# A decoder block on one core, its instruction order written out as a table

## The chip, the core and the metric

The kernel runs on one core of one Trainium2 chip. The metric is device time in microseconds from the start to the end of one execution. The core has a matrix engine (TensorE, shown as PE, with its weight loads as PEld), a vector engine (VectorE, DVE), a scalar and lookup engine (ScalarE, ACT), GpSimd (POOL), and SyncE (SP), which here only issues DMA transfers. Each engine works through its own list of instructions in order and waits at semaphores for the others. Transfers are issued by SP, ACT and POOL; a transfer that has to wait for its operand or its buffer holds up everything behind it on the engine that issues it. Matmul results go to PSUM, of which the kernel uses eight banks under the names ps_A, ps_B, ps_C and ps_D.

## What is computed

One decoder layer for 512 tokens of width 1024 in float32:

```python
h = h + 0.5 * swiglu(rmsnorm(h), ffn1_w1, ffn1_w3, ffn1_w2)   # hidden width 2816
z = rmsnorm(h) @ w_in             # 8 queries, 3 x (2 keys, 2 values), gates, S5 input u
o_nsa = nsa_attention(q, ...)     # 8 heads x 64: compressed, selected and window branch
o_s5  = s5_mixer(u, ...)          # 32 groups x 16 channels, 64 complex states, scan over 512
h = h + concat(o_nsa, o_s5) @ w_out
h = h + 0.5 * swiglu(rmsnorm(h), ffn2_w1, ffn2_w3, ffn2_w2)
h = h + sigmoid(rmsnorm(h) @ w_gate) * (p @ w_ple)            # p has width 256
out = rmsnorm(h)
```

With eight selected blocks out of eight the selected branch sees all earlier keys, so it is a causal attention like the window branch; the compressed branch attends to 31 pooled blocks. S5 is a linear recurrence, followed by gelu and a gated projection (GLU, `glu`).

## The kernel before

Activations stand transposed, channels on partitions and tokens in columns: `h` is eight tiles of 128x512. A product in float32 precision is made of three matmuls in the faster fp32r type: every operand is split into a rounded part and a rest (`hi` and `lo` for weights, `xh` and `xl` or `sh` and `sl` for activations, `hq` for hidden tiles), and hi*hi, hi*lo and lo*hi are added in PSUM. For each unit of 128x1024 weights this means a load (`raw<-in_wpack`, line 111), a cast on ACT (`hi<-raw`, line 152) and a subtraction on DVE (`lo<-raw,hi`, line 154). All matmuls go through one helper, line 131.

**Feed-forward.** 22 hidden tiles are made and consumed in four chunks (`CHUNKS`, `FFN_ORDER`): `up` makes a hidden tile, `down` adds a chunk's product to `h` (line 488). After the first seven tiles of the first feed-forward, and the first two of the second, the tiles are "fast" (`up_fast`): they use seven half products instead of eight, from sums and differences of weight halves. These sums are made by two accumulating transfers, which POOL issues (lines 362 and 368), and two DVE additions (lines 364 and 365); ACT's `ah` (line 370) and DVE's `al` (line 371) split the last. Partial products are copied between banks by ACT (lines 383 and 399), combined by DVE into `t3` (lines 422, 426 and 432, shown as `t` by the profile), and split into `hq` (lines 352 and 353).

**Mixer.** Queries, keys and values are projected and rotated; the rotated queries go to DRAM (`qd<-r`) and come back in another layout (`qf<-qd`, lines 1147 and 1148); keys and values for the compressed branch go the same way (`kcd`, `vcd`, then `cst`, lines 1044 and 1045). ACT copies the returned queries into `QA` and `QB` (lines 1149 and 1150). `scores` finds the row maxima of the scores; `values` then walks over 48 blocks of keys: score matmuls into ps_B or ps_C, one exponential into `e`, a second rounded one into `eh` (every third a DVE copy instead), a DVE subtraction `el` (line 1264), and two matmuls into ps_D. S5 runs beside it, with its state passed through DRAM by POOL (`si`, `so`). After the gelu of S5 (`yt`, line 871), `glu` multiplies by gate weights and `out_half(4-8)` projects S5's half of the output; `out_half(0-4)` projects attention's half when its last piece (`oh`, `ol`, lines 1275 and 1276) is ready.

**What sets the order.** The program is written with generators that are woven in fixed proportions (`weave`), with a few instructions pinned in place (`tc.keep_in_program_order`, `tc.issue_after`); from that, the framework's planner (`schedule_with_timeline_sim=True`) decides the order on each engine. Weight units are loaded by SP in the feed-forwards and by ACT in the mixer; the choice is this line:

```python
load_unit(i, q or (nc.sync if more else nc.scalar))
```

Raw units come from a ring of four buffers (a larger ring where `more` is set), so a load waits until the unit that had the buffer before has been split.

Of the kernel before, what the change touches and what calls it, by code (L numbers as in the profile page):

```python
# [76 lines left out]
def block_kernel(ctx: ExitStack, tc: tile.TileContext, a: dict, out: bass.AP):  # L77
# [22 lines left out]
    raws, loads = {}, {}  # L100
# [3 lines left out]
    def load_unit(i, q):  # L104
        w = UNIT_W[i]
        if more and i % (4 + more[1]) >= 4:
            raw = more[0].tile([128, UNIT], F32, tag="raw", name="raw", bufs=more[1])
        else:
            raw = ring.tile([128, UNIT], F32, tag="raw", name="raw", bufs=4)
        src = a["wpack"][128 * UNIT_OFF[i]:128 * UNIT_OFF[i + 1]].rearrange("(p c) -> p c", c=w)  # L110
        loads[i] = q.dma_start(raw[:, :w], src)
        raws[i] = raw
# [15 lines left out]
    pinned = tc.keep_in_program_order  # L128
# [7 lines left out]
    def unit(raw_only=False, keep=None, q=None, after=None):  # L136
        i = unit_i[0]
        unit_i[0] += 1
        w = UNIT_W[i]
        if i not in raws:  # L140
            load_unit(i, q or (nc.sync if more else nc.scalar))
        raw = raws.pop(i)
        if raw_only:
            return raw
        return split(raw, (slice(0, 512), slice(512, w)) if i == 0 else (slice(0, w),), keep, after)

    def split(raw, parts=(slice(0, UNIT),), keep=None, after=None):
# [3 lines left out]
        for c in parts:  # L151
            S.copy(hi[:, c], raw[:, c])  # L152
            with tc.issue_after(after.ins) if after else nullcontext():
                V.tensor_tensor(lo[:, c], raw[:, c], hi[:, c].bitcast(F32), OP.subtract)  # L154
# [11 lines left out]
    class Norm:  # L166
# [25 lines left out]
        def finish(self, pin=False):  # L192
            self.ri, pb = rsqrt_rows([self.acc], 4, pin)
            self.rb = npool.tile([128, SEQ], F32, tag="rb", name="rb", bufs=1)
            V.tensor_copy(self.rb, pb)
# [57 lines left out]
    class Scaled(Norm):  # L253
# [13 lines left out]
        def spread(self, tmp, xpool, pool, pb):  # L267
# [8 lines left out]
            def scale(k):  # L276
                pinned(V.scalar_tensor_tensor(row(k), h[:, k, :], gains[:, self.gi, k:k + 1], pb, OP.mult, OP.mult))
                S.copy(self.xh[:, k], row(k))

            for k in range(KT + 1):  # L280
                if k < KT:
                    scale(k)
                if k:
                    self.last = pinned(V.tensor_tensor(self.xl[:, k - 1], row(k - 1),
                                                       self.xh[:, k - 1].bitcast(F32), OP.subtract))
# [4 lines left out]
            def combine(n, a, b, op):  # L290
                t = tmp().rearrange("p a (b c) -> p (a b) c", c=256)
                with tc.issue_after(self.last.ins):
                    for i in range(2):
                        V.tensor_tensor(t[:, 2 * i:2 * i + 2], a(i), b(i), op)
# [12 lines left out]
    def rsqrt_rows(parts, nb, pin=False):  # L307

        steps = rsqrt_steps(parts, nb, pin)
# [3 lines left out]
    def rsqrt_steps(parts, nb, pin=False, pin_last=False):  # L313
        st = bank("D", (128, 4))[:, :nb]
        for b in range(nb):
            for i, t in enumerate(parts):
                p = mm(st[:, b:b + 1], t[:, b * 128:(b + 1) * 128], ones[:, 0:1], i == 0, i == len(parts) - 1)
                if pin and b + i == 0:
                    pinned(p)
# [11 lines left out]
        p = mm(pb, ones, dg.rearrange("p b t -> p (b t)"), True, True)  # L331
        if pin_last:
            pinned(p)
# [10 lines left out]
    def ffn(nrm, done, plain, xp, hp, fp, bg=None, first=None, restate=None):  # L344
        fast = not bg
        if True:
# [88 lines left out]
            def up(f):  # L435
                if f >= plain:
                    return up_fast(f, f + 1 < FT_N and f not in [c[0] for c in CHUNKS[1:]])
                after = nrm.last if fast and f == 0 else None
                wu = [first if f == 0 and first else unit(), unit(after=after)]
                z = [bank("C"), bank("C")] if f == 2 else [bank("A"), bank("B")]  # L440
                both = [(j, k) for j in range(2) for k in range(KT)]
                if after:
# [29 lines left out]
            def aside(n, mark=None):  # L472
                for _ in range(n if bg else 0):
                    with tc.issue_after(mark.ins) if mark else nullcontext():
                        next(bg, None)

            def down(fl, last):
                n = len(fl)
                cur = None
                for m in range(KT):  # L480
# [7 lines left out]
                    mark = V.scalar_tensor_tensor(h[:, m, :], o, 0.5, h[:, m, :], OP.mult, OP.add)  # L488
# [5 lines left out]
                    if not last:  # L494
                        aside((2 - m % 2) * (m > 4 or fl[0] > 0), mark)
# [18 lines left out]
    def s5_constants(sp):  # L514
        if True:
# [10 lines left out]
            late(bx, a["s5_b"])  # L526
            cx = sp.tile([128, 2, NG, 16], F32, name="cx")
            late(cx, a["s5_c"])
            dk = sp.tile([16, NG], F32, name="dk")
            late(dk, a["s5_dT"])  # L530
            sgn = sp.tile([128, 2], F32, name="sgn")
            late(sgn, a["sgn"])
# [275 lines left out]
    def mixer(ctx):  # L808
# [50 lines left out]
        table = []  # L859

        def act(*args, **kw):
            with tc.issue_after(table[0].ins):
                S.activation(*args, **kw)  # L863

        def gelu2(o, x, w, tag):

            t = tp.tile([128, SEQ], F32, tag=tag, name="gt")[:, :w]
            act(t, x, AF.Square)
            V.scalar_tensor_tensor(t, t, 1 / 0.044715, x, OP.add, OP.mult)
            act(t, t, AF.Tanh, scale=math.sqrt(2 / math.pi) * 0.044715)  # L870
# [146 lines left out]
        def v_gates():  # L1017
# [18 lines left out]
            act(gp1, gp1, AF.Exp)  # L1036
# [60 lines left out]
        def glu():  # L1097
# [4 lines left out]
            for m in range(4):  # L1102
# [8 lines left out]
                act(sg, o, AF.Tanh, scale=0.25, bias=bglu[:, m:m + 1])  # L1111
# [23 lines left out]
        def scores(qb, env, pool, tags="B", stage=("ra", "ra")):  # L1135
# [24 lines left out]
            for j, (h0, b0) in enumerate((h0, b0) for half in range(2) for b0 in range(0, 2, nb)  # L1160
# [9 lines left out]
                for i in range(n):  # L1170
                    for r in range(nb):
                        act(s_[:, i, r], s_[:, i, r], AF.Exp, bias=mc[:, i, r:r + 1], accum_out=dc[:, i, r:r + 1])
                yield

        def compressed(*qbs):

            for qb in qbs:
# [14 lines left out]
                act(ec, ec, AF.Exp)  # L1192
# [38 lines left out]
        def values(qb, env):  # L1231
# [3 lines left out]
            for g in range(2):  # L1235
# [5 lines left out]
                for i, (br, kb) in enumerate(blocks):  # L1241
# [16 lines left out]
                    act(e, st, AF.Exp)  # L1258
                    if i % 3 == 2:
                        V.tensor_copy(eh, e)  # L1260
                    else:
                        act(eh, st, AF.Exp)
# [41 lines left out]
        table.append(tc.keep_in_program_order(S.preload_act_table_set("exp_and_others")))  # L1304
# [80 lines left out]
    norm2 = rsqrt_steps([n2.acc], 4, True, True)  # L1385
    for m in range(KT):
# [23 lines left out]
    with tc.tile_pool(name="gate", bufs=2, reuse_waits="tile") as gp:  # L1410
# [12 lines left out]
        for hf in range(2):  # L1423
            cs = slice(hf * HS, hf * HS + HS)
            for i in range(KT):
# [8 lines left out]
                if i == 0 and hf == 0:  # L1434
                    ng.finish(True)
# [37 lines left out]


# [149 lines left out]
```

## Time and profile before

| | us |
|---|---|
| median of 3 runs | 1095.41 (1093.74 to 1097.05) |
| the profiled execution | 1096.0 |
| its span, first to last instruction | 1094.2 |
| TensorE busy in the span | 1042.1 |
| VectorE busy | 794.0 |
| ScalarE busy | 516.8 |
| GpSimd busy | 92.7 |
| mean granted TensorE clock | 0.985 of full |

The views used below are these. The page's first part gives each engine's busy time. A table by stretches gives, for each piece of the span, the busy time of every engine with its number of instructions, the granted clock, the busy share of the DMA engines and the rate. Waits are listed by engine, tile and source line, with the instruction that ended them: "PE ps_A L131 <- DVE yt L871: 5.8, 1, 5.8" means that matmuls into ps_A waited 5.8 us in all, once, at longest 5.8 us, for DVE's `yt` of line 871. The chain of waits goes back from the last instruction, each step to what released it. In timeline rows a bracket such as [5.87 <-ACT ps_B L863] gives the idle time before the instruction and what ended it. Matmuls are pipelined, so their shown length is longer than their spacing.

### The profile page before, as it was taken

Reading aid. Unit: us, or ns where it says so; the run is one execution under the profiler, and the core shown is the slowest. Engines: PE = TensorE matmul, PEld = TensorE weight load, DVE = VectorE, ACT = ScalarE, POOL = GpSimd, SP = SyncE. Lnnn points to the kernel's source line nnn. Section 1 sums busy time; section 2 is a strip of 40 time slices with the busy share of each in tenths; the row PEclk is TensorE's granted clock in tenths of the full one; section 3 lists DMA queues with packets and bytes.
Section 4 is the critical chain, followed back from the end, with each engine's and each line's share of the span. In section 5 each row is a group of like instructions: output and inputs, shape, how many; then the busy total and the mean of one; then the engine's idle time right before and its main releaser. Section 6 shows DMA issues by size and latency. Waiting matters only on the chain.

```text
span 1094.2 us, 16835 instructions
## 1 busy us (share of the span) xinstructions
PE 1042.1 (95%) x6446; PEld 897.5 (82%) x6446; DVE 794.0 (73%) x1339; ACT 516.8 (47%) x911; POOL 92.7 (8%) x118
## 2 busy tenths in 40 slices
PE   6999999998999999979799999999999999999996
PEld 4887999798889788767377668799899899898895
DVE  6999786786787766777468887976477557566766
ACT  5334255344435423346647875555255245255541
POOL 5000010000000200010000001011010101000000
PEclk9999999999999999989899999999999999999998
DMA  9334366786657737773621026256365635535302
GB/s 284 137 99 112 81 166 171 192 200 153 166 130 187 234 97 226 216 218 111 187 68 40 0 97 173 77 146 176 84 144 142 177 73 143 171 96 153 111 8 77
DMA packets 86625, 151.14 MB, mean 138 GB/s; under 512 B 27648, under 2 KB 47104, under 8 KB 86544
## 3 DMA queue, kind: packets, MB, share of 16 engines
q1 hardware_dynamic: 66352, 98.11, 29.5%
q0 software_dynamic: 13152, 29.66, 13.7%
q10 hardware_dynamic: 7040, 22.29, 6.5%
q8 instruction: 50, 0.82, 0.3%
q14 instruction: 31, 0.25, 0.1%
HBM read 123.27 MB, written 17.83 MB: 129 GB/s over the span
## 4 chain that ended last, share of the span: by engine, by line
PE 62%; ACT 4%; issue 3%; DVE 3%; DMA 3%; ACTq 0%; SPq 0%; POOLq 0%; POOL 0%; DVEq 0%
PE ps_A L131 18%; PE ps_C L131 18%; PE ps_B L131 17%; PE ps_D L131 10%; DMA qf<-qd 2%; ACT e L863 1%; ACT eh L863 1%; ACT ps_B L863 1%; DMA raw<-in_wpack 1%; DVE el L1264 0%; DVE lo L154 0%; ACT hi L152 0%; DMA qd<-r 0%; ACT QA L1149 0%; ACT pt L1270 0%
## 5 line engine op out<-in xcount | busy, mean ns | idle before, releaser
L152 ACT CAST hi<-raw 128x1024 fp32r<-128x1024 f32 (+2 forms) x201 | 206.0, 1041 | 245.8 <-PE ps_C L131 103.5
L154 DVE TENSOR_TENSOR lo<-raw,hi 128x1024 fp32r<-128x1024 f32 (+2 forms) x201 | 240.0, 1218 | 70.8 <-ACT hi L152 66.4
L131 PE MATMUL ps_C<-hq,hi 128*128 128x512 f32 x704 | 218.0, 392 | 3.9 <-ACT hq L352 2.3
L131 PEld LDWEIGHTS ps_C<-hq,hi 128*128 128x128 f32 x704 | 130.4, 188 | 32.9 <-ACT hq L352 3.2
L131 PE MATMUL ps_A<-xh,hi 128*128 128x256 f32 (+1 forms) x456 | 141.0, 311 | 7.4 <-ACT xh L175 6.3
L131 PE MATMUL ps_A<-xl,hi 128*128 128x256 f32 (+1 forms) x456 | 141.2, 312 | 3.1 <-DVE xl L176 2.1
L131 PE MATMUL ps_A<-xh,lo 128*128 128x256 f32 (+1 forms) x456 | 140.9, 310 | 1.7 <-DVE lo L154 1.7
L131 PE MATMUL ps_C<-hq,lo 128*128 128x512 f32 x352 | 136.2, 390 | 0.0
L131 PEld LDWEIGHTS ps_A<-xh,hi 128*128 128x128 f32 x456 | 86.4, 190 | 12.7 <-ACT xh L175 6.2
L131 PEld LDWEIGHTS ps_A<-xl,hi 128*128 128x128 f32 x456 | 86.2, 190 | 11.6 <-DVE xl L176 4.7
L131 PEld LDWEIGHTS ps_A<-xh,lo 128*128 128x128 f32 x456 | 86.4, 190 | 6.2 <-DVE lo L154 1.9
L131 PE MATMUL ps_B<-sh,hi 128*128 128x256 f32 x280 | 79.1, 283 | 2.7 <-ACT ps_B L399 2.7
L131 PE MATMUL ps_B<-sh,lo 128*128 128x256 f32 x280 | 78.8, 281 | 0.7 <-DVE lo L154 0.7
L131 PE MATMUL ps_B<-sl,hi 128*128 128x256 f32 x280 | 78.9, 282 | 0.0
L131 PEld LDWEIGHTS ps_C<-hq,lo 128*128 128x128 f32 x352 | 66.1, 188 | 13.6
L362 POOL DMA_DIRECT2D raw<-in_wpack x35 | 30.4, 869 | 483.7 <-DVE h L1127 168.3
L488 DVE SCALAR_TENSOR_TENSOR h<-ps_C,h 128x512 f32<-128x512 f32 x64 | 43.9, 689 | 36.8 <-PE ps_C L131 36.4
L131 PE MATMUL ps_D<-sh,hi 128*128 128x256 f32 x220 | 61.7, 283 | 0.4 <-ACT hi L152 0.4
L131 PE MATMUL ps_D<-sh,lo 128*128 128x256 f32 x220 | 61.7, 281 | 0.0
L131 PE MATMUL ps_D<-sl,hi 128*128 128x256 f32 x220 | 61.3, 281 | 0.0
L131 PE MATMUL ps_B<-xh,hi 128*128 128x512 f32 (+1 forms) x164 | 57.9, 353 | 0.9 <-ACT hi L152 0.9
L131 PE MATMUL ps_B<-xh,lo 128*128 128x512 f32 (+1 forms) x160 | 56.0, 350 | 0.8 <-DVE lo L154 0.8
(402 smaller groups left out, 2327.4 us busy)
## 6 DMA issues: line engine op xcount, KB each, us to landing
raw<-in_wpack SPq DMA_DIRECT2D x132, 512.0 KB, 4.3
raw<-in_wpack ACTq DMA_DIRECT2D x40, 512.0 KB, 4.2
raw<-in_wpack POOLq DMA_DIRECT2D x35, 256.0 KB, 4.2
raw<-raw POOLq DMA_DIRECT2D x35, 256.0 KB, 3.4
so<-s5o POOLq DMA_DIRECT2D x8, 768.0 KB, 5.9
si<-s5i POOLq DMA_DIRECT2D x8, 512.0 KB, 5.6
h<-in_xT SPq DMA_DIRECT2D x8, 256.0 KB, 5.5
s5i<-fs SPq DMA_DIRECT2D x4, 512.0 KB, 4.6
```

Source lines behind the costliest of these rows:

```text
L131: return PE.matmul(o, lhsT, rhs, start=start, stop=stop, **kw)
L152: S.copy(hi[:, c], raw[:, c])
L154: V.tensor_tensor(lo[:, c], raw[:, c], hi[:, c].bitcast(F32), OP.subtract)
L362: nc.gpsimd.dma_start(a0[:, 1], src[:, 0:512], accum_op=OP.add)
L488: mark = V.scalar_tensor_tensor(h[:, m, :], o, 0.5, h[:, m, :], OP.mult, OP.add)
L863: S.activation(*args, **kw)
```

## The change

The planner's order is replaced. A table, `ENGINE_ORDER`, lists for each engine its instructions in the wanted order, as runs of steps through the program as it was traced; a second, `TILE_ORDER`, lists pairs of instructions for tiles that share a buffer. The new function `impose` turns each neighbouring pair of the table into a dependency, which the planner has to keep. All pins of the old program are taken out, and every weight unit is loaded by SP. That moves 43 loads from ACT's list to SP's; the other instructions stay on their engines. The arithmetic is the same: the same matmuls, splits and transfers are issued.

```diff
-    def unit(raw_only=False, keep=None, q=None, after=None):
+    def unit(raw_only=False, keep=None):
...
         if i not in raws:
-            load_unit(i, q or (nc.sync if more else nc.scalar))
+            load_unit(i, nc.sync)
...
-            def late(dst, src):
-                with tc.issue_after(loads[7].ins):
-                    nc.sync.dma_start(dst, src)
-
             prm = t32("prm", 3)
-            late(prm, a["s5_prm"])
+            nc.sync.dma_start(prm, a["s5_prm"])
...
-        def act(*args, **kw):
-            with tc.issue_after(table[0].ins):
-                S.activation(*args, **kw)
...
-        table.append(tc.keep_in_program_order(S.preload_act_table_set("exp_and_others")))
+        S.preload_act_table_set("exp_and_others")
...
-                pinned(mm(o, w_[:, sl], x_, k + i == 0, k == 1 and i == 2))
+                mm(o, w_[:, sl], x_, k + i == 0, k == 1 and i == 2)
...
+ENGINE_ORDER = {
+    "PE": (
+        "65:15 9:2 -11:7 4:5 -9:2 7:10 7:3 -10:5 5 -6:2 25:20 -32 31 3:2 -5 4:6 -10:2 8:15 21:18 6:3 -9:4 5:3 -8 "
...
+TILE_ORDER = (
+    "49>792 395>1091 604>948 2341>2357 3185>3260 3186>3261 3225>4160 3281>3594 3468>3731 3532>3556 3533>3561 "
...
+def impose(tc):
+
+    traced = list(tc.nc.cur_bb.bb.instructions)
+    follow = mybir.DependencyInfo(mybir.DependencyClass.NoSync, mybir.DependencyReason.DATA)
+    for moves in ENGINE_ORDER.values():
+        at, before = 0, None
+        for move in moves.split():
+            step, _, count = move.partition(":")
+            at += int(step)
+            for _ in range(int(count or 1)):
+                if before is not None:
+                    tc.add_manual_dep(traced[at], before.name, follow, reason="order")
+                before = traced[at]
+                at += 1
+    for pair in TILE_ORDER.split():
+        a, b = map(int, pair.split(">"))
+        tc.add_manual_dep(traced[b], traced[a].name, follow, reason="order of tiles")
...
     with tile.TileContext(nc, schedule_with_timeline_sim=True) as tc:
         block_kernel(tc, aps, out)
+        impose(tc)
```

What this does to the lists of single engines is shown at three places. In these listings every tile carries the number of its buffer, the same number in both programs.

POOL's list in the first feed-forward, near its fast tiles at 240 to 270 us. Line 362 or 354 adds the second unit of a tile to the first while loading it; line 368 or 360 is the accumulation that follows after both are split. Before:

```order
L362 DMA raw_2381<-in_wpack 128x512
L368 DMA raw_2122<-raw_2120 128x512
L362 DMA raw_2533<-in_wpack 128x512
L368 DMA raw_2255<-raw_2253 128x512
L362 DMA raw_2659<-in_wpack 128x512
L368 DMA raw_2383<-raw_2381 128x512
L368 DMA raw_2535<-raw_2533 128x512
```

And now:

```order
L354 DMA raw_2381<-in_wpack 128x512
L360 DMA raw_2122<-raw_2120 128x512
L360 DMA raw_2255<-raw_2253 128x512
L354 DMA raw_2533<-in_wpack 128x512
L360 DMA raw_2383<-raw_2381 128x512
L354 DMA raw_2659<-in_wpack 128x512
L360 DMA raw_2535<-raw_2533 128x512
```

The accumulation into raw_2383 stood behind the load of raw_2659, and now stands ahead of it.

SP's list in the mixer, where the second group of queries (qf_4704) returns from DRAM; kcd and vcd are the stores of the compressed branch's keys and values, and cst their loads. Before:

```order
L1008 DMA kcd_3797<-ra_4343 64x512 x2
L1013 DMA vcd_3798<-ra_4450 128x512
L1147 DMA qf_4704<-qd_3795 64x4x128
L1148 DMA qf_4704<-qd_3795 64x4x128
L1044 DMA cst_5046<-kcd_3797 64x512
L1045 DMA cst_5046<-kcd_3797 64x511
L1044 DMA cst_5049<-kcd_3797 64x512
L1045 DMA cst_5049<-kcd_3797 64x511
```

And now:

```order
L988 DMA kcd_3797<-ra_4343 64x512
L111 DMA raw_5079<-in_wpack 128x1024
L993 DMA vcd_3798<-ra_4450 128x512
L111 DMA raw_5085<-in_wpack 128x1024
L1127 DMA qf_4704<-qd_3795 64x4x128
L1025 DMA cst_5049<-kcd_3797 64x511
L1024 DMA cst_5049<-kcd_3797 64x512
L1025 DMA cst_5046<-kcd_3797 64x511
L1024 DMA cst_5046<-kcd_3797 64x512
L1128 DMA qf_4704<-qd_3795 64x4x128
```

Two weight loads have come in from ACT's list, and the second half of qf_4704 has moved behind the four loads of cst.

TensorE's list where the first value block of the attention begins: ps_D_5310 is its output, ps_C_5374 and the following ps_C are scores, and ps_A_5333 and ps_A_5516 are the output projection of the S5 half. Before:

```order
L131 MATMUL ps_B_5573<-KB_3803,QB_5116 128x256
L131 LDWEIGHTS identb_88
L131 MATMUL ps_B_5573<-maskq_3809,identb_88 128x128
L131 MATMUL ps_D_5310<-eh_5316,VLc_3805 128x512
L131 MATMUL ps_C_5374<-QA_4297,KA_3802 128x512
L131 MATMUL ps_C_5374<-QB_4298,KB_3803 128x512
L1227 MATMUL ps_D_5396<-ident_86,cc_5265 48x128
L131 MATMUL ps_D_5310<-el_5319,VLc_3805 128x512
L131 MATMUL ps_D_5310<-eh_5357,VL_3804 128x512
```

And now:

```order
L130 MATMUL ps_C_5385<-QA_4297,KA_3802 128x512
L130 MATMUL ps_C_5409<-QA_4297,KA_3802 128x512
L130 MATMUL ps_A_5333<-oh_3855,hi_5336 128x512
L130 MATMUL ps_A_5333<-ol_3856,hi_5336 128x512
L130 MATMUL ps_D_5310<-eh_5316,VLc_3805 128x512
L130 MATMUL ps_C_5385<-QB_4298,KB_3803 128x512
L130 MATMUL ps_A_5333<-oh_3855,lo_5337 128x512
L130 MATMUL ps_D_5310<-el_5319,VLc_3805 128x512
L130 MATMUL ps_D_5310<-eh_5357,VL_3804 128x512
L130 MATMUL ps_D_5310<-el_5360,VL_3804 128x512
```

The output projection, which before had been done for its first row some 200 instructions earlier, now stands between score and value matmuls, one matmul at a time.

More of the change, by code (lines that the diff above doesn't have):

```diff
@@ L1 @@
 import math
-from contextlib import ExitStack, nullcontext
+from contextlib import ExitStack
 import numpy as np
@@ L99, in block_kernel @@
     nc.scalar.dma_start(gains, a["gains"])
-    raws, loads = {}, {}
+    raws = {}
     more = []
@@ L110, in load_unit @@
         src = a["wpack"][128 * UNIT_OFF[i]:128 * UNIT_OFF[i + 1]].rearrange("(p c) -> p c", c=w)
-        loads[i] = q.dma_start(raw[:, :w], src)
+        q.dma_start(raw[:, :w], src)
         raws[i] = raw
@@ L144, in unit, with split @@
             return raw
[L145 to L147 removed]
+        return split(raw, (slice(0, 512), slice(512, w)) if i == 0 else (slice(0, w),), keep)
+    def split(raw, parts=(slice(0, UNIT),), keep=None):
         pool, n = (keep, 5) if keep else (ring, 3)
@@ L152, in split @@
             S.copy(hi[:, c], raw[:, c])
-            with tc.issue_after(after.ins) if after else nullcontext():
-                V.tensor_tensor(lo[:, c], raw[:, c], hi[:, c].bitcast(F32), OP.subtract)
+            V.tensor_tensor(lo[:, c], raw[:, c], hi[:, c].bitcast(F32), OP.subtract)
         return hi, lo
@@ L291, in combine @@
                 t = tmp().rearrange("p a (b c) -> p (a b) c", c=256)
-                with tc.issue_after(self.last.ins):
-                    for i in range(2):
-                        V.tensor_tensor(t[:, 2 * i:2 * i + 2], a(i), b(i), op)
+                for i in range(2):
+                    V.tensor_tensor(t[:, 2 * i:2 * i + 2], a(i), b(i), op)
                 hi = pool.tile([128, 4, 256], FR, name=f"sh{n}")
@@ L437, in up @@
                     return up_fast(f, f + 1 < FT_N and f not in [c[0] for c in CHUNKS[1:]])
-                after = nrm.last if fast and f == 0 else None
-                wu = [first if f == 0 and first else unit(), unit(after=after)]
+                wu = [first if f == 0 and first else unit(), unit()]
                 z = [bank("C"), bank("C")] if f == 2 else [bank("A"), bank("B")]
                 both = [(j, k) for j in range(2) for k in range(KT)]
-                if after:
+                if fast and f == 0:
                     both = [(j, k) for k in range(KT) for j in range(2)]
@@ L470, in up, with aside @@
                         next(restate, None)
-            def aside(n, mark=None):
+            def aside(n):
                 for _ in range(n if bg else 0):
-                    with tc.issue_after(mark.ins) if mark else nullcontext():
-                        next(bg, None)
+                    next(bg, None)
             def down(fl, last):
@@ L1472 @@
 PADS = 320, 0, 224, 24832
+ENGINE_ORDER = {
[105 rows of a table added]
+    ),
+    "DVE": (
[40 rows of a table added]
+    ),
+    "ACT": (
[28 rows of a table added]
+    ),
+    "POOL": (
[5 rows of a table added]
+    ),
[12 rows of a table added]
+    ),
+}
+TILE_ORDER = (
[6 rows of a table added]
+)
+def impose(tc):
[14 more added lines that the diff above has]
+        tc.add_manual_dep(traced[b], traced[a].name, follow, reason="order of tiles")
 def _pack_weights(x):
```

57 lines of the change are left out of this document (25 added, 32 removed), and 193 rows, old and new, of tables (ENGINE_ORDER, TILE_ORDER).

## The prediction

> **What bounds the kernel now.** First the page's busy table, then the granted clock and busy time by stage, then what TensorE waited for.
>
> ```profile
> PE 1042.1 (95%) x6446; PEld 897.5 (82%) x6446; DVE 794.0 (73%) x1339; ACT 516.8 (47%) x911; POOL 92.7 (8%) x118
> ```
>
> TensorE is busy 95% of the span, so the whole prize is the rest, plus the time in which it was "busy" at a low clock. The next view cuts the span into stretches (start:end, length, then busy time of PE, PEld, DVE, ACT and POOL with instruction counts, granted clock, DMA share, GB/s).
>
> ```profile
> 0.00:20.00 20.00, 10.66 (x33) 6.68 (x34) 14.33 (x13) 13.48 (x21) 13.29 (x16) 1.00 0.91 297
> 261.00:265.00 4.00, 0.89 (x6) 0.48 (x4) 2.03 (x4) 2.80 (x5) 0.00 (x0) 1.00 0.44 119
> 265.00:269.00 4.00, 3.92 (x22) 3.92 (x23) 4.00 (x13) 1.60 (x4) 0.86 (x1) 0.63 0.57 161
> 456.00:476.00 20.00, 12.78 (x105) 9.90 (x105) 14.34 (x34) 8.23 (x20) 2.11 (x4) 0.87 0.84 259
> 528.00:538.00 10.00, 3.06 (x11) 1.40 (x10) 6.89 (x11) 8.95 (x20) 0.00 (x0) 0.71 0.66 184
> 538.00:549.00 11.00, 11.00 (x29) 4.79 (x29) 4.06 (x6) 4.63 (x10) 0.00 (x0) 0.79 0.40 126
> 586.00:648.00 62.00, 58.77 (x268) 39.48 (x267) 55.41 (x118) 55.29 (x136) 0.00 (x0) 1.00 0.08 25
> 538.00:648.00 110.00, 106.27 (x492) 72.93 (x493) 86.01 (x181) 76.76 (x188) 0.00 (x0) 0.98 0.15 46
> 693.00:1000.00 307.00, 307.00 (x2152) 287.72 (x2151) 199.15 (x257) 141.57 (x226) 32.02 (x37) 1.00 0.51 133
> 1081.00:1094.20 13.20, 2.40 (x10) 1.54 (x10) 5.63 (x17) 0.83 (x2) 0.70 (x1) 0.66 0.24 79
> ```
>
> The body of the second feed-forward (693 to 1000) has no idle time: no order can improve it. The losses are islands: start, 261 to 269, 456 to 476, 528 to 549, the attention that ends at 648, and the last 13 us. In the attention DVE and ACT are each busy 55 of 62 us, so there it is those two, not TensorE, that a new order must feed. TensorE's waits name the late partners (total, times, longest):
>
> ```profile
> PE ps_B L131 <- ACT ps_B L863: 7.4, 4, 5.9
> ...
> PE ps_A L131 <- DVE yt L871: 5.8, 1, 5.8
> PE ps_B L131 <- ACT ps_B L399: 2.7, 1, 2.7
> PE ps_C L131 <- ACT hq L352: 2.3, 2, 1.2
> PE ps_A L131 <- DVE xl L176: 2.1, 3, 0.7
> ...
> PE ps_A L131 <- DVE lo L154: 1.7, 1, 1.7
> ...
> PE ps_B L131 <- DVE t L426: 1.0, 1, 1.0
> PE ps_A L131 <- DVE gt L1437: 0.9, 1, 0.9
> ```
>
> To turn a stretch of the new order into time I use the spacing of matmuls in undisturbed runs of the chain of waits:
>
> ```profile
> 763.32 23.37 PE ps_C L131 x103
> ...
> 793.65 1.42 PE ps_B L131 x12
> ```
>
> That is 0.227 us for 512 columns and 0.118 for 256. Below, "PE work" is matmuls in order times this spacing.
>
> **The change, part by part.** No operation is removed; 43 weight loads change queue and every engine's order changes. The sum is made against the profiled execution: 1096.0 us, 1.8 beside its span of 1094.2, and 0.6 above the median of 1095.41.
>
> *Start.* Seven fills of the zeroed state now stand on SP ahead of the second hidden tile's weights; before they stood behind them.
>
> ```profile
> 9.38 9.62 SPq L663 DMA_DIRECT2D s5o<-zz  x7
> ...
> 6.25 0.79 PE L131 MATMUL ps_A<-xh,hi 128*128 128x512 f32 x1 [6.25 <-ACT xh L175]
> ...
> raw<-in_wpack SPq DMA_DIRECT2D x132, 512.0 KB, 4.3
> ```
>
> Issuing them took 9.6 us. The loads of the input, of three weight units and of the small state tables stand ahead of them; at the 0.4 to 0.6 us that such an issue takes on SP these end near 8 us. So the second tile's weights go out near 17.7 us, land some 4.3 later, perhaps 6 behind the fills, and need a cast and a subtraction: ready between 23.5 and 25. TensorE wants them after 11.8 us of PE work, at 6.25 + 11.8 + 5 = 23 us, where the 5 are the waits of the start less a part. Against this the second bank's matmuls are interleaved with the first's, which fills part of the 2.1 us of waits on xl. I take +0.5 (bounds -2 and +3). The 13 us at the end are a chain whose order is the same: 0.
>
> *Edges of the feed-forward tiles.* The largest is at 264. POOL (GpSimd) issues in order, and the second row below stood behind the first, which waited for a buffer; ACT's cast `ah` waited for that second transfer, and the copy that TensorE needed stood behind the cast:
>
> ```profile
> 255.45 0.86 POOL L362 DMA_DIRECT2D raw<-in_wpack  x1 [11.19 <-DVE lo L154]
> 255.99 1.22 POOL L368 DMA_DIRECT2D raw<-raw  x1
> ...
> 252.89 2.57 DVE L154 TENSOR_TENSOR lo<-raw,hi 128x1024 fp32r<-128x1024 f32 x2 [0.60 <-ACT hi L152]
> ...
> 262.20 0.62 ACT L370 CAST ah<-raw 128x512 fp32r<-128x512 f32 x1 [5.20 <-DMA raw<-raw]
> ...
> 264.09 0.39 PE L131 MATMUL ps_B<-sh,hi 128*128 128x256 f32 x1 [2.70 <-ACT ps_B L399]
> ```
>
> The new POOL order puts the second ahead of the first; the subtraction that reads the same buffer (`lo`) ended near 254.2, so the transfer could have gone out 1.5 us before 255.99. ACT's order at that place is unchanged, so what is late next is still the cast, by about 1 us. The stall also cost clock: 0.63 over 265 to 269 is 1.5 us. All edges together: 2.7 + 1.5 here, 1.0 (t), 2.3 (hq), 1.7 (lo) and 0.9 (gt) from the waits, 10.1 us. I take 8, since the new order interleaves two tiles at each of them; bounds 2 (the POOL swap alone) and 12 (with the weight-load waits that lie beside them).
>
> *The stall at 468.* ACT's copies of the next queries stand ahead of the exponential that TensorE needs, and these queries come through DRAM:
>
> ```profile
> 474.15 0.79 PE L131 MATMUL ps_B<-KA,QA 128*128 128x512 f32 x1 [5.87 <-ACT ps_B L863]
> ...
> 471.39 0.63 ACT L1150 ACTIVATE QB<-qf 64x512 fp32r<-64x512 f32 x1 [6.44 <-DMA qf<-qd]
> ...
> 460.78 0.62 SPq L1147 DMA_DIRECT2D qf<-qd  x1
> 461.45 0.66 SPq L1148 DMA_DIRECT2D qf<-qd  x1
> 462.22 0.93 SPq L1044 DMA_DIRECT2D cst<-kcd  x1
> ...
> 464.46 1.15 SPq L1045 DMA_DIRECT2D cst<-kcd  x1
> ...
> 461.45 11.19 DMA qf<-qd
> ```
>
> ACT keeps this order. The last row, from the chain of waits, is the landing of the second half, 11.2 us. The load now starts earlier against TensorE: between the projection that SP's preceding store waits for and the stalled matmul lie 19.4 us of PE work instead of 13.8, 5.6 more. But the second half of qf now stands behind four cst loads, which, with what came between, were issued over 462.22 to 465.6, and these land late (size, us from issue to landing in 436 to 476):
>
> ```profile
> cst<-kcd SPq DMA_DIRECT2D x2, 128.0 KB, 12.3
> raw<-in_wpack ACTq DMA_DIRECT2D x4, 512.0 KB, 4.9
> ```
>
> That takes back 3.4 us. The stall is then 5.9 - 5.6 + 3.4 = 3.7 us; with the clock lost behind it (0.87 over 20 us is 2.6) reduced by a third, 2.2 + 0.9, I take -3. Bounds: -8.5 (stall and clock all gone), +4 (two more weight loads of 512 KB ahead at 259 GB/s, 2 us each, and the second half landing with the cst).
>
> *The stall at 532.* TensorE waited for the last gelu output:
>
> ```profile
> 537.73 1.22 PE L131 MATMUL ps_A<-yt,raw 128*128 128x512 f32 x1 [5.84 <-DVE yt L871]
> ```
>
> The new order spreads these matmuls over other work and brings forward the compressed keys, but a serial chain of gelu, transposes and small matmuls now precedes yt on DVE: about six hops of 0.4 to 0.7 us, 3.5 us. I take -2.5 (bounds 0 and -5.8).
>
> *Attention.* From yt to the last output piece DVE has 86.0 us of work in 110; the new order leaves 1.5 us more for this stretch, 87.5. TensorE's own share falls to 81 us, because the first value blocks start where out-projection matmuls still are available to mix in, and ACT's is 77. So DVE sets the end. At the 55.4 of 62 that it reaches today in the densest part (89%) the stretch takes 98; fully packed 87.5. I take 96, -14, since from its first microsecond it now has work that doesn't wait for the gate matmuls (4.06 busy of 11 in 538 to 549 today). Bounds -22.5 and 0 (the old 78%). That ACT no longer issues 43 loads frees it, but ACT is not the fullest here, so I cost this at nothing; if DVE were not the cover, ACT's 77 us would still leave 19 of the 96.
>
> Sum: 1096.0 + 0.5 - 8 - 3 - 2.5 - 14 = 1069; on the median's level, **1068 us**.
>
> **Rivals.** (1) SP's list eats half (0.20). All loads now share one list with waits on stores: the 468 term goes to +4 and the out-projection weights come late, so attention keeps only -7: 1068 + 7 + 7 = 1082. For it: qf took 11 us from issue with only SP's own traffic ahead, while weights on ACT's list landed in 4.9. Against: most weight loads stand far ahead of use. The Trainium skill, "DMA: Bandwidth & Descriptors" (section "Queues, rings and completion order"), supports it: rows are served in turn, one row's ring in order. The 4.9 beside 12.3 agrees.
>
> (2) Packed (0.15): DVE full in attention (-8.5 more), 468 gone (-5.5), all edges (-4): 1050. For it: the orders come from durations like these. Against: no engine exceeds 95% of such a stretch today.
>
> (3) Slower (0.08): in the feed-forward bodies single matmuls of different banks alternate, and TensorE runs in order, so one that waits holds up ready ones of the other bank. The fast tiles number 35, one for each such load:
>
> ```profile
> raw<-in_wpack POOLq DMA_DIRECT2D x35, 256.0 KB, 4.2
> ```
>
> If each stalls by the 1.0 us of the `t` wait, the time is 1068 + 35 = 1103. It decides where the margin between lo and its matmul falls below zero; the busy 307 of 307 shows a margin now, and the new order stays within 2 us of PE work of the old there.
>
> (4) Clock (0.05): with DVE as the bound, TensorE waits in many short pieces in attention, 15 of 96 us, and the granted clock falls as it did between 528 and 549, to a mean of 0.75. Then its 81 us become 108, 12 more than DVE's 96: 1080. Against it stands the row of 586 to 648, where 3 us of short waits left the clock at 1.00; for it, 261 to 269, where waits of 3.2 us in 4 brought it to 0.63. The Trainium skill, "TensorE: Matmul & The Clock Gate" (section "A second HAM failure mode: psum-queue depth-cycling"), tells of just this: frequent short idles between groups of matmuls make the clock swing between half and full. At the density of idle that these rows show, the trace does not bear it out.
>
> (5) No effect (0.02), 1095: the listed orders differ on all engines, so hardly.
>
> **Numbers.** The forecast has 0.50, and its own range is 1058 to 1080: 10 us below for an attention at 95% of DVE with half of the 468 stall gone, 12 above for one at DVE's present 89% with edges of 4 and a start of +3. A measurement of this kernel can tell 0.3%, 3.3 us, from no change. Faster: 0.50 + 0.15 + 0.05 and most of the first rival, 0.17 of its 0.20, is 0.87. Same: the rest of it and the fifth, 0.05. Slower: 0.08. The range of 1050 to 1091 reaches from the packed case to the far side of rival 1 and leaves out rival 3, the fifth and half of the packed one, 0.18.
>
> **What would show it.** Right: DVE above 88% busy for some 95 us before the out-projection's second half; yt's wait under 4 us; the qf wait of ACT about 4 us; no 2.7 us wait on L399's successor; bodies still without idle. Wrong: first, qf waits of 8 us and more; second, under 2 us and DVE above 96%; third, new waits on lo or hi of 1 us all over the bodies. A start longer than 9.3 us of lost time in the first 20 would refute the first term, and idle TensorE with DVE below 80% in attention the largest.

## The result: 0.85% slower, and the profile after

The changed kernel took 1104.34 us (median of 4 runs, 1102.6 to 1105.7) against 1094.58 for the kernel before (4 runs): a ratio of 1.0085, with a 95% interval of 1.0062 to 1.0108. The forecast of 1068 us and its range of 1050 to 1091 both missed, on the wrong side of no change. The profiled execution spans 1102.4 us, 8.2 more than before.

The first part of the page after, busy time by engine, and below it the list of what TensorE waited for (total, times, longest; us). In this kernel the matmul helper is line 130, `hi` 151, `lo` 152, `ah` 362, `yt` and `ht` 851.

```profile
PE 1064.6 (97%) x6446; PEld 904.8 (82%) x6446; DVE 809.3 (73%) x1339; ACT 521.1 (47%) x911; POOL 94.8 (9%) x118
```

```profile
PE ps_A L130 <- ACT xh L173: 7.0, 1, 7.0
PE ps_D L130 <- DVE dg L322: 3.1, 2, 2.1
PE ps_B L130 <- DVE lo L152: 2.9, 3, 2.2
PE ps_A L130 <- DVE xl L174: 2.8, 4, 1.6
PE ps_B L130 <- ACT ah L362: 1.7, 2, 1.2
...
PE ps_B L130 <- ACT hi L151: 1.6, 1, 1.6
...
PE ps_C L1055 <- DVE ht L851: 1.2, 1, 1.2
```

The waits at 264, 468 and 532 us that the forecast set out to shorten are gone from this list: no 5.9 on the exponential, no 5.8 on `yt`, no 2.7 behind the copy of line 399. TensorE idles 37.8 us instead of 52.1 (span less busy). Yet the kernel is longer, and "busy" grew by 22.5 us for the same 6446 matmuls. So the loss lies inside what the profile calls busy. The table by stretches shows it (start:end, length, busy time and count of PE, PEld, DVE, ACT and POOL, granted clock, DMA share, GB/s), first after, then two rows of before:

```profile
0.00:20.00 20.00, 9.92 (x28) 6.69 (x29) 14.56 (x13) 12.55 (x20) 13.49 (x16) 1.00 0.88 286
80.00:90.00 10.00, 6.20 (x20) 4.38 (x19) 9.44 (x29) 2.61 (x4) 0.00 (x0) 0.83 0.32 106
700.00:1000.00 300.00, 299.40 (x2063) 276.21 (x2062) 189.78 (x241) 133.92 (x214) 30.95 (x36) 1.00 0.48 126
440.00:480.00 40.00, 40.00 (x237) 31.73 (x236) 28.06 (x56) 14.38 (x28) 2.22 (x4) 1.00 0.82 217
526.00:536.00 10.00, 7.85 (x68) 5.18 (x68) 7.18 (x14) 8.41 (x23) 0.00 (x0) 1.00 0.36 105
536.00:546.00 10.00, 10.00 (x53) 5.79 (x51) 4.28 (x11) 8.21 (x18) 0.00 (x0) 0.83 0.36 106
```

```profile
80.00:90.00 10.00, 10.00 (x46) 8.29 (x45) 9.95 (x27) 5.04 (x9) 0.00 (x0) 1.00 0.19 55
700.00:1000.00 300.00, 300.00 (x2122) 281.95 (x2121) 192.15 (x249) 136.74 (x220) 32.02 (x37) 1.00 0.51 131
```

Two things are new. At 80 to 90 us TensorE, full before, now is busy 6.2 of 10 and loses clock. And in the second feed-forward both kernels are "busy" 100% at full clock, but 300 us hold 2063 matmuls instead of 2122. The 59 missing ones, at 300/2122 = 0.14 us each, are 8 us. Busy TensorE hardly moved, and the other engines' columns fell with the matmuls, the weight loads' (PEld) from 281.95 to 276.21. The Trainium skill, "Perfetto Trace Analysis" (section "Identifying the Most-Contended Engine"), warns of just this: busy time of matmuls doesn't measure the distance from the roofline (the best that the hardware allows), and the arithmetic done per time and the busy share of weight loads are to be read instead. The two rows agree.

To place the whole difference I charged each matmul with the median distance from its start to the next start for its shape, over the two traces. What a stretch takes beyond that sum is its lost time; because the sum runs over the same matmuls in both kernels, stretches can be compared although their clock times have shifted. Lost us, by stretch of matmul work (60 us of work lie near 73 us of the old trace, 440 near 467, 500 near 545, 520 near 569, 640 near 708, 920 near 988):

| matmul work, us | before | after | after less before |
|---|---|---|---|
| 0 to 60 (start) | 13.0 | 15.7 | +2.7 |
| 60 to 440 (first feed-forward) | 14.2 | 20.2 | +6.0 |
| 440 to 500 (the waits at 468 and 532) | 17.4 | 6.9 | -10.5 |
| 500 to 520 | 4.4 | 8.3 | +3.9 |
| 520 to 640 (attention, out-projection, norm) | 18.8 | 14.5 | -4.3 |
| 640 to 920 (body of the second feed-forward) | 0.6 | 9.2 | +8.6 |
| 920 to 1006 (its end, the tail) | 6.1 | 7.5 | +1.4 |
| all | 74.5 | 82.3 | +7.8 |

Single traces of one and the same order differ by up to 2 us in a row of this table. The picture is larger than that: the mixer gains 10.9 us, and the feed-forwards and the start lose 18.7.

**The wait at 80 to 90 us.** Timeline rows of the kernel after; the bracket is the idle time before the instruction and what ended it:

```profile
81.13 0.62 ACT L344 CAST hq<-t 128x512 fp32r<-128x512 f32 x1 [4.00 <-DVE t L457]
81.66 1.04 ACT L151 CAST hi<-raw 128x1024 fp32r<-128x1024 f32 x1
...
82.39 0.39 DVE L578 SCALAR_TENSOR_TENSOR sn<-sn,phs 128x224 f32<-128x224 f32 x1
82.69 1.24 DVE L584 SCALAR_TENSOR_TENSOR cs<-cs,phs 128x224 f32<-128x224 f32 x3
...
82.75 0.51 PE L130 MATMUL ps_B<-xh,hi 128*128 128x512 f32 x1 [1.56 <-ACT hi L151]
...
83.85 0.68 DVE L454 TENSOR_TENSOR t<-ps_A,rb 128x512 f32<-128x512 f32 x1
84.45 1.22 DVE L152 TENSOR_TENSOR lo<-raw,hi 128x1024 fp32r<-128x1024 f32 x1
...
85.72 0.79 PE L130 MATMUL ps_B<-xh,lo 128*128 128x512 f32 x1 [2.24 <-DVE lo L152]
```

`hi` of this weight unit was ready at 82.7: on ACT its cast stood behind the cast `hq`, which had waited 4.00 us for DVE's `t`. DVE, busy 38.6 us of the 40 to 80, had four rows of sine and cosine tables for S5 ahead of `t` and `lo`, so `lo` came at 85.7 and TensorE stood for it. The clock of the next microseconds fell with it (0.83 over the 10 us).

**The late tenths.** The weight loads' own waits in 700 to 1000 us. For the kernel before, this list is empty; after, it begins:

```profile
PEld ps_B L130 <- ACT ah L362: 0.9, 1, 0.9
PEld ps_C L130 <- issue: 0.7, 2, 0.4
PEld ps_B L130 <- DVE lo L152: 0.5, 3, 0.2
PEld ps_B L130 <- issue: 0.5, 2, 0.3
PEld ps_D L130 <- ACT p L375: 0.3, 1, 0.3
PEld ps_A L130 <- DVE lo L152: 0.2, 1, 0.2
```

One of them, in the timeline (all engines; PEld are the weight loads):

```profile
716.45 1.23 DVE L152 TENSOR_TENSOR lo<-raw,hi 128x1024 fp32r<-128x1024 f32 x1
...
717.38 0.28 PE L130 MATMUL ps_D<-sh,lo 128*128 128x256 f32 x1
717.38 0.19 PEld L130 LDWEIGHTS ps_D<-sh,hi 128*128 128x128 f32 x1
717.50 0.28 PE L130 MATMUL ps_D<-sh,hi 128*128 128x256 f32 x1
...
717.73 0.19 PEld L130 LDWEIGHTS ps_B<-sh,lo 128*128 128x128 f32 x1 [0.16 <-DVE lo L152]
717.73 0.39 PE L130 MATMUL ps_B<-sh,lo 128*128 128x256 f32 x1
...
717.96 0.28 PE L130 MATMUL ps_B<-sh,hi 128*128 128x256 f32 x1
```

In step, a weight load starts with the matmul before its own (717.38), and matmuls follow every 0.12 us. Here `lo` ended at 717.68 (716.45 and 1.23), 0.18 us late, so its load could not start with the matmul at 717.50: it starts only with its own matmul, and that and the next are spaced by 0.23 us each instead of 0.12. Two matmuls lose 0.22 us together, and no row of PE shows idle time.

For every wait of TensorE in 700 to 1000 us, take as slack the start of the matmul ahead less the end of the instruction waited for. Before, 224 waits had a median slack of 2.20 us and none was below 0.2. After, 194 have a median of 0.67; 48 are below zero, and with the matmul behind each they hold 8.25 of the stretch's 9.4 us of lost time, 0.17 each. The largest holders are `lo` (15 times, 1.9 us), ACT's copies `pu` and `p` (25, 2.9) and DVE's `t3` (7, 1.1).

### The profile page after: what moved, and what is told of

It reads as the page before. It is cut to its first block, busy times and chain, and to the rows that moved or that the text cites. A ratio compares the mean times of both kernels' runs of the same rounds, so it can differ in the third digit from the quotient of the medians.

```text
span 1102.4 us, 16831 instructions
## 1 busy us (share of the span) xinstructions
PE 1064.6 (97%) x6446; PEld 904.8 (82%) x6446; DVE 809.3 (73%) x1339; ACT 521.1 (47%) x911; POOL 94.8 (9%) x118
## 3 DMA queue, kind: packets, MB, share of 16 engines
q0 software_dynamic: 13152, 29.66, 13.4%
## 5 line engine op out<-in xcount | busy, mean ns | idle before, releaser
L152 DVE TENSOR_TENSOR lo<-raw,hi 128x1024 fp32r<-128x1024 f32 (+2 forms) x201 | 243.3, 1218 | 82.5 <-ACT hi L151 62.9
L130 PE MATMUL ps_C<-hq,lo 128*128 128x512 f32 x352 | 133.1, 391 | 0.0
L130 PEld LDWEIGHTS ps_A<-xh,hi 128*128 128x128 f32 x456 | 87.2, 192 | 14.2 <-ACT xh L173 7.0
L478 DVE SCALAR_TENSOR_TENSOR h<-ps_C,h 128x512 f32<-128x512 f32 x64 | 44.1, 690 | 52.7 <-PE ps_C L130 52.1
L130 PE MATMUL ps_B<-sh,hi 128*128 128x256 f32 x280 | 81.8, 292 | 0.0
L130 PEld LDWEIGHTS ps_C<-hq,lo 128*128 128x128 f32 x352 | 66.0, 188 | 12.6
```

Of the source, the lines that this page charges most:

```text
L130: return PE.matmul(o, lhsT, rhs, start=start, stop=stop, **kw)
```

## The experiments

Each kernel is timed against the kernel before, which ran beside it with medians of 1095.7 to 1098.2 us; differences in microseconds are therefore taken from the ratios, 0.1% being 1.1 us. There are two kinds of experiments: tables put together from both orders, cut at times of the old trace; and reliefs of DVE and ACT that leave out part of the arithmetic. In what follows, "lost" is the measure of the table above.

**The old order as a table, all loads on SP.** All five lists of the table hold the old order; the 43 moved loads are merged into SP's by their old times. Of the changed lines of the tables (122 to 379) only the first is shown here and below.

```diff
 ENGINE_ORDER = {
     "PE": (
-        "65:15 9:2 -11:7 4:5 -9:2 7:10 7:3 -10:5 5 -6:2 25:20 -32 31 3:2 -5 4:6 -10:2 8:15 21:18 6:3 -9:4 5:3 -8 "
+        "65:18 6:2 -8 7:17 -24:3 21:3 -24:2 22:2 25:2 -27:4 23:34 -48 47:12 20:48 26:2 22:2 -24:22 2:22 12:48 "
...
```

> The change's mechanism with the old order: every engine's list is the old kernel's, written as a table, and only the 43 weight loads of the mixer move from ACT to SP, placed among SP's transfers by the times at which ACT issued them. Theory A (the loss comes from the new order): 1093 to 1097 us, as before. Theory B (the loss comes from putting all loads on SP's list, or from the table as such): slower than before by most of the 8 to 10 us, 1102 to 1105, with longer waits of ACT on qf.

Measured: 1097.45 us, ratio 1.0004 [0.9987, 1.0022]. Neither the form of a table nor the moved queue costs anything that can be measured. The whole difference is the new order.

**The new order in the mixer alone.** The same edit, with the old rows up to 455 us and from 712 us of the old trace and the new ones between.

> Old order up to 455 us and from 712 us of the old trace, the new order between (mixer and second norm); loads on SP. Theory A: measured against matmul work the new order lost 8.7 us up to the mixer and 10 after it, and gained 10.9 between; so this kernel takes 1094.6 - 11 = 1084 us, with room of 2 for the seams. Theory B: the mixer holds all 43 moved loads, so it would carry the loss: 1095 or more.

Measured: 1088.09 us, ratio 0.9910 [0.9890, 0.9929], 9.9 us below the kernel before, of the 11 that theory A expected.

**The old order in the second feed-forward.** The changed kernel with the old rows from 712 us on:

```diff
 ENGINE_ORDER = {
     "PE": (
...
-        "37:7 -15:3 12:2 -14 13 21 -22:6 -20 19:4 12:4 8:3 -11:3 8:3 -11:3 8:6 -14 -13 -11 55:2 -17:10 7:6 14:3 "
+        "37:7 -15:3 12:2 -14 13 21 -22:6 -20 19:4 12:4 8:3 -11:3 8:3 -11:3 8:6 -14 -13 -11 40:12 51:12 -39:3 "
...
```

> The changed kernel with the old order from 712 us of the old trace on (second feed-forward and end). Theory A: 10 us of its loss lie there, so 1104.3 - 10 = 1094 to 1095 us, and the many small waits of TensorE between 700 and 1000 us vanish. Theory B: 1102 or more, since nothing moved between queues in this stretch.

Measured: 1095.86 us, ratio 0.9986 [0.9972, 1.0001], 1.0% below the changed kernel. The body of the second feed-forward loses 1.3 us instead of 9.2.

**The old order in the first feed-forward.** The old rows up to 455 us, the new ones behind.

> The changed kernel with the old order up to 455 us of the old trace (start, first feed-forward, first projections). Theory A: 8.7 us of the loss lie there, of them 5.9 at 82 to 90 us, so 1095 to 1096 us. Theory B: 1102 or more.

Measured: 1097.45 us, ratio 1.0007 [0.9988, 1.0027], 0.8% below the changed kernel. What each stretch loses comes out as in the kernel that its order is from: 16.1 in 60 to 440 (14.2 before), 8.9 in 640 to 920 (9.2 after), both within the 2 us by which single traces differ. Stretches add up.

**Pieces.** Six cuts, so that the wait at 264 and the end of the second feed-forward are taken from the new order too.

> The table is put together from pieces of both orders, cut at the old trace's times: old order up to 243 us, new from 243 to 373, old to 460, new from 460 to 708 (mixer, attention, out-projection, second norm), old to 986, new to 1013, old to the end. Theory A (each stretch has its own cost, and what the change loses it loses in the feed-forward stretches): the gains of the new order stand without its losses. Against the kernel before: stretch 460 to 708 gains 10.9 us by the stage accounting of the two profiles, 243 to 373 gains about 5 (the wait at 264), 986 to 1013 about 1.7: 17.6 us less than before, ratio 0.984. Theory B (stretches depend on each other, a stretch that begins with another's order pays at the seam): each of six seams costs about 1 us or more, and the result is no better than the kernel with only the mixer new, ratio 0.991 or above.

Measured: 1083.98 us (4 runs), ratio 0.9885 [0.9846, 0.9924]: 12.6 us below the kernel before, and the fastest of all. The sum had promised 17.6. Its trace (span 1082.8) accounts for 11.7: 440 to 500 loses 9.4 where the new order alone loses 6.9, the start loses 14.2 where the old order on all engines loses 13.0 to 13.4, and 220 to 240, just ahead of a cut, 2.4 where each order alone loses 0.3 or 1.1. So theory A holds for the sum's sign and most of its size, and the seams cost some microseconds, as theory B had it.

**The old front.** The changed kernel with the old rows up to 114 us.

> The changed kernel with the old order up to 114 us of the old trace (the start and the first state steps, with the new wait at 82 to 90 us), the new one behind it. Theory A (the wait at 82 to 90 us is made by the order in that place, where DVE computes tables for later ahead of what TensorE needs): the losses up to there go, 1.5 at the start and 5.9 at the wait, 7.5 us less than the changed kernel: 1097 on the median's level. Theory B (the work that DVE did there is only shifted, and makes a wait of that size later): at most 2 us less, 1102 or more.

Measured: 1096.41 us, ratio 1.0007 [0.9988, 1.0025], 0.8% or 8.5 us below the changed kernel's ratio. The first 100 us of matmul work lose 14.2 us as before instead of 21.8, and no wait of that size comes later. The order at that place made the wait.

**The weights' low part by a copy.** DVE's subtraction is replaced by a copy, in the new order and, as a control, in the old one:

```diff
             S.copy(hi[:, c], raw[:, c])
-            V.tensor_tensor(lo[:, c], raw[:, c], hi[:, c].bitcast(F32), OP.subtract)
+            V.tensor_copy(lo[:, c], hi[:, c].bitcast(F32))
```

> The changed kernel, where the low part of every weight is a copy of the high part (DVE 0.8 instead of 1.22 us for each of 160 units, ready 0.4 us earlier; this leaves out the low part of the weights). Theory A (in the feed-forward bodies the new order has used up the margin, so that what DVE and ACT deliver late by tenths of a microsecond holds TensorE up): the loss in 640 to 1000 us of matmul work falls from 16 us by a third or more, and the whole by 8 to 15 us. Theory B (the loss comes from TensorE's own sequence, the alternating of banks and of weights, and would stand with producers in time): the loss in that stretch stays within 2 us, and the whole within 4 us, of the changed kernel's.

> The old order written as a table, with the low part of every weight a copy of the high part (0.68 instead of 1.22 us on DVE for each unit of 128x1024; this leaves out the low part of the weights). The same edit took 16 us from the changed kernel, and 5.8 of the 16.8 us lost in 640 to 1006 us of matmul work. Theory A (the new order has used up a margin that the old one has): the old order gains little, within 1.5 us of 6.7 lost in 640 to 1006, and 5 us or less in the whole against the old table without the edit (1097.5). Theory B (a faster DVE helps any order of this kernel, so that the gain says nothing of the margin): 10 us or more in the whole.

Measured, new order: 1089.54 us, ratio 0.9941 [0.9923, 0.9959], 15.8 us below the changed kernel's ratio. Old order: 1088.32 us (4 runs), ratio 0.9915 [0.9888, 0.9942], 9.8 us below the old table without the edit; its trace accounts for 6.6 of them. The copy took 0.68 us instead of 1.22, more relief than expected. Rows of the new order with the copy:

```profile
80.00:90.00 10.00, 9.24 (x41) 7.64 (x42) 9.21 (x38) 4.58 (x7) 0.00 (x0) 1.00 0.31 102
```

```profile
700.00:1000.00 300.00, 299.94 (x2082) 278.13 (x2081) 148.11 (x243) 135.56 (x218) 31.49 (x35) 1.00 0.52 135
```

| lost us, by matmul work | old order | old, copy | new order | new, copy |
|---|---|---|---|---|
| 60 to 440 | 14.5 | 11.3 | 20.2 | 11.3 |
| 640 to 920 | 0.6 | 0.6 | 9.2 | 6.4 |
| 920 to 1006 | 6.1 | 5.0 | 7.5 | 4.5 |

In the feed-forwards the relief gives the new order 14.7 us and the old one 4.3, so 10.4 of the 16.0 us that the new order loses there go with it. With it, the two lose the same 11.3 in the first, and the wait at 80 to 90 is down to 1.2. The old order's body of the second gains nothing: there it had margin to spare. So producers that are late made most of the loss, as theory A says; but a faster DVE also helps the old order more than theory A allowed, and nearly as much as theory B asked (9.8 us, against 5 and 10; the trace shows 6.6, with 4.3 in the feed-forwards and the rest at the start and in the mixer). Part of the gain of 15.8 is therefore no evidence: by the times the new order gains 6.0 us more than the old, uncertain by some 5, and the 10.4 rest on the traces. Of the new order's body 6.4 us stay, mostly at waits for ACT's copies and `hi`, which the edit doesn't hasten; that these would go with a faster ACT was not tried and is not shown.

**The attention: DVE relieved.**

```diff
-                    V.tensor_tensor(el, e, eh.bitcast(F32), OP.subtract)
+                    V.tensor_copy(el, eh.bitcast(F32))
```

> The changed kernel, where the 48 subtractions that give el (the low part of the attention's exponentials) are replaced by copies of the high part on the same engine: 0.42 instead of 0.69 us each, 13 us less work for DVE in the attention; this leaves out the low part of the exponentials. The forecast's claim (DVE sets the end of the attention): the attention gets about 10 us shorter, the whole 1094. The rival (DVE was busy only 83% of that stretch, TensorE waits in order for a chain through ACT and DVE, and the number of engine hops sets the pace): less than 3 us, 1101 or more.

Measured: 1101.99 us, ratio 1.0057 [1.0033, 1.0080], 3.1 us below the changed kernel's ratio for 13 us less of DVE's work. Both ratios are uncertain by 0.23%, so this gain is hardly clear of none, and it is far from the 10 us that the forecast's claim asks for. DVE does not set the end.

**DVE and ACT relieved, in both orders.**

```diff
-                    S.activation(e, st, AF.Exp)
+                    if i % 3 == 2:
+                        S.activation(e, st, AF.Exp)
+                    else:
+                        S.activation(e[:, :16], st[:, :16], AF.Exp)
...
-                    V.tensor_tensor(el, e, eh.bitcast(F32), OP.subtract)
+                    V.tensor_copy(el, eh.bitcast(F32))
```

> The changed kernel with both partners of the attention relieved: el is a copy of eh on DVE (0.42 instead of 0.69 us, 48 times), and where ACT computes eh itself, its first exponential e is cut to 16 columns (about 0.2 instead of 0.60 us, 32 times), so eh is ready 0.4 us earlier and ACT has some 13 us less work, DVE 13 us; this leaves out the low part of the exponentials and most of e. Theory A (TensorE waits in order for a chain of ACT, DVE and TensorE per block, and late exponentials and el make the lost time): the stretch of 500 to 640 us of matmul work loses 22.8 us in the changed kernel and 21.0 with only DVE relieved; it falls to 16 or less, the whole to 1099 or less on the median's level where the changed kernel has 1105. Theory B (what is lost there lies in TensorE's own sequence, in short matmuls and changes of weights, and in the chain ahead of the attention): no less than 19.5, the whole 1102 or more.

> The same relief of DVE and ACT in the old order written as a table (1097.5 without the relief; the same parts left out). Its stretch of 500 to 640 us of matmul work loses 23.2 us. Theory A (late exponentials make the lost time; in the old order 24 late eh, 15 late el and 5 late e carried 8.4 us of it, in the new order 10, 10 and 6 of them 3.4 us): the old order gains more than the new, 6 us or more. Theory B (TensorE's own sequence): less than 3 us in both. Theory C (the forecast: a partner's total work sets the end of the attention, DVE's in the new order, and it is now 13 us less in both): 10 us or more in both.

Measured, new order: 1100.14 us, ratio 1.0030 [1.0012, 1.0047], 6.0 us below the changed kernel's ratio. Old order: 1095.00 us, ratio 0.9957 [0.9940, 0.9974], 5.2 us below the old table's. The row of 525 to 640 us in the changed kernel, with DVE relieved, and with both relieved:

```profile
525.00:640.00 115.00, 109.86 (x540) 73.92 (x540) 95.92 (x198) 92.88 (x223) 0.00 (x0) 0.99 0.16 47
```

```profile
525.00:640.00 115.00, 111.11 (x547) 75.65 (x546) 85.40 (x199) 93.46 (x222) 0.00 (x0) 0.99 0.17 48
```

```profile
525.00:640.00 115.00, 111.58 (x548) 77.35 (x544) 85.78 (x200) 81.17 (x219) 0.00 (x0) 0.99 0.19 54
```

Ten microseconds off DVE and twelve off ACT bring TensorE 8 more matmuls into 115 us. In lost time of 500 to 640 us of matmul work the new order goes from 22.8 to 21.0 and 19.2, the old one from 24.7 to 18.7. Theory C, the forecast's, falls: it asked for 10 us or more in both. Between the other two the runs don't decide. By the traces the old order gains more (6.0 us against 3.6), as theory A has it; by the times it doesn't (5.2 against 6.0, each uncertain by some 3), and the new order's 19.2 and 1100.14 lie between the limits of both theories. With both partners relieved this far, some 19 us stay lost in that stretch in either order. What makes them is not settled: in the new order waits met late by TensorE carry 8.7 of the 18.8 us lost from 546 to 646, most of them small and from at least nine different producers; the other 10 us lie at matmuls that no late wait precedes.

## Why the prediction was wrong

| term | forecast, us | lost time after less before, us |
|---|---|---|
| start | +0.5 | +2.7 |
| edges and bodies of the feed-forwards | -8 | +16.0 (+6.0 +8.6 +1.4) |
| stalls at 468 and 532 | -5.5 | -6.6 (-10.5 +3.9) |
| attention | -14 | -4.3 |
| sum | -27 | +7.8 |

**Edges and bodies: the step that failed most.** The step is the cost of nothing for the bodies, where the runs show a loss. The forecast read "busy 307 of 307" as a margin and let the bodies cost nothing, and named the opposite only as its third rival, with 0.08. The named edges did gain: the wait at 264 went from 5.4 us lost to 0.8, and the weak places of 300 to 340 us of matmul work from 4.3 to 1.2. GpSimd's order changed as read, with `raw<-raw` now ahead:

```profile
251.99 0.86 POOL L360 DMA_DIRECT2D raw<-raw  x1 [11.14 <-DVE lo L152]
253.08 0.87 POOL L354 DMA_DIRECT2D raw<-in_wpack  x1 [0.23 <-issue]
```

That is 7.7 us, close to the 8. But the new order spent the margin elsewhere: 5.9 us at 80 to 90, a place that the forecast never looked at because no idle time stood there, and about 18 more over both feed-forwards (16.0 + 7.7 - 5.9), which the count of slack puts mostly on lateness by tenths: in 700 to 1000 us 8.25 of 9.4, in 100 to 440 us 8.3 of 11.3 (there with single waits of 1.4 and 1.2 us among them). The third rival had the mechanism right, with "where the margin between lo and its matmul falls below zero", and the size wrong: not one stall of 1.0 us per fast tile, 35, but 0.17 us at each of many small waits, about half of that in all. The alternation of banks costs nothing by itself: in the feed-forward bodies, matmuls without a wait nearby that follow one of another bank start 0.6 ns late on average (769 pairs), and those of the same bank 0.2 ns. Being late costs, as the rival said. "Within 2 us of PE work of the old" was no comfort, since 2.2 us was the old order's median slack.

**Attention: the second.** DVE's 87.5 us were taken as the end of the stretch. From yt to the last output piece the stretch did shrink, from 113.7 to 107.6 us by the starts of these two on DVE (before 537.0 to 650.7, after 538.1 to 645.7). DVE was busy 95.9 of the 115 us above (83%), and from 546 to 646 it all but reached the 88% that the forecast had named as the sign of being right:

```profile
546.00:646.00 100.00, 97.01 (x444) 67.19 (x443) 87.69 (x178) 77.34 (x184) 0.00 (x0) 1.00 0.14 43
```

Yet relieving it of 13 us gave 3. The sign nearly came true and the mechanism did not: a busy share doesn't tell what sets the end. TensorE's "81 us" were an error too: the matmuls between those two points amount to 86.1 us at their undisturbed spacing (89.0 before), and 21.5 us of waits, clock and lost overlap come on top (24.7 before). An engine at 81 of 96 us is not out of the way if its work comes in a chain of hops with two partners.

**The stalls: right.** The first, with -3, was undersized: TensorE is busy 40 of 40 us at 440 to 480, and 440 to 480 us of matmul work lose 3.5 us instead of 8.1, -4.6. No 11 us landing of `qf` came; the loads' medians in 436 to 480 us are

```profile
raw<-in_wpack SPq DMA_DIRECT2D x4, 512.0 KB, 5.6
...
qf<-qd SPq DMA_DIRECT2D x10, 128.0 KB, 5.4
```

so the 3.4 us that the forecast gave back to the `cst` loads, and with them the first rival (SP's list), are refuted; the old order with all loads on SP says the same. The second stall went as described: no 5.8 on `yt`, but `ht` (1.2) and `chid` (0.9) of the serial chain, and a clock of 0.83 in 536 to 546. Its -2.5 stands against 13.6 lost in 480 to 520 us of matmul work before and 11.7 after, -1.9.

**Start:** right in sign by luck, short by 2 us, inside its bounds. The wait that it was made of, for the second tile's weights behind the fills, did not come: the loss lies ahead of it, where the first `xh` came 0.7 us later (6.96 against 6.25) and the first `xl` wait took 1.6. By the forecast's own sign, more than 9.3 us without matmuls in the first 20, the term fails: there are 10.1 (9.92 of 20 busy). The kernels with all loads on SP and the old front lose 13.0 to 13.4 in the first 60 us of matmul work, so it is the order, not the queue.

**Clock rival:** the granted clock was 1.00 in 546 to 646 and 0.989 over the span; it played no part there.

**The range:** the bounds of the forecast's own case, 1058 to 1080, don't follow from what they name. Below, 87.5 / 0.95 is 92 us, 4 less than 96, and half of the 5.5 us left of the 468 stall and its clock is 2.75: 7 us, not 10. Above, 98 us for the attention, edges of 4 and a start of +3 make 2 + 4 + 2.5 = 8.5, not 12. The measured time lies outside by either reckoning.

## What to carry to other kernels

A stretch that shows 100% busy, with its matmuls at their undisturbed spacing, has next to nothing to gain from a reordering (0.6 us in the old body here) and its whole slack to lose: before moving an order through it, read each producer's end against the start of the matmul ahead of its user, and count the margin, not the idle time. Judge such a stretch by matmuls per microsecond and by the weight loads' waits, since lateness of tenths hides inside "busy": the new body shows 299.40 of 300 us and loses 9. And where stretches add up as they do here, take the order only where the old one has waits to give: the pieces of both reached 0.9885 of the old time, the whole new order 1.0085.

## What the runs showed of the hardware

- A weight that was ready 0.18 us after the start of the matmul ahead cost 0.22 us: its load no longer hid behind that matmul, and two matmuls were spaced 0.23 us instead of 0.12 (the rows at 717.7).
- Two waits of 1.56 and 2.24 us, 0.7 us of matmuls between them, went with a granted clock of 0.83 over 80 to 90; with the same place cut to one wait of 0.87 us (the kernel with the weights' low part by a copy) it stayed at 1.00.
- Replacing DVE's subtraction of 128x1024 by a copy brought it from 1.22 to 0.68 us, 128x512 from 0.69 to 0.42.
